# Split weights moved by 384 bytes, a seven-product scheme on two or four chunks by group, and plain products in the last two blocks

## The chip, the cores and the metric

The kernel runs on one core of a Trainium2 chip. The metric is the device time of one execution in microseconds (us). Before the change it is 1715.49 us, the median of three runs (1714.62 to 1716.32). The engines in this text are TensorE (PE; its weight loads, which overlap the matmuls, stand apart as PEld), VectorE (DVE), ScalarE (ACT), GpSimd (POOL) and SyncE (SP), which issues most DMAs. L132 is line 132 of the kernel before. On-chip memory (SBUF) has 128 partitions; an address is a byte offset within a partition. Matmuls accumulate in PSUM.

## The reference

One layer of a decoder for 256 tokens of width 2048 in float32: a combined projection, three token mixers (gated linear attention, stick-breaking attention, cross-attention into 256 memory tokens), a gated merge, an output projection, and a gated feed-forward block of width 5632.

```python
h = rmsnorm(x, attn_norm)
gq, gk, gv, gr, ga1, sq, sk, sv, mq, gates = split(h @ w_in)
y_gla = (rmsnorm(gla(gq, gk, gv, ga1)) * silu(gr)) @ w_br_gla
y_sb  = stick_breaking(rmsnorm(sq), rmsnorm(sk), sv) @ w_br_sb
y_mem = memory(rmsnorm(mq), rmsnorm(mem) @ w_mem_kv) @ w_br_mem
g = sigmoid(gates)                       # three gates of 2048 channels
x = x + (g0 * y_gla + g1 * y_sb + g2 * y_mem) @ w_o
gate, up = split(rmsnorm(x, ffn_norm) @ w_gate_up)
x = x + (silu(gate) * up) @ w_down
```

## The kernel before

**Tiling.** The 256 tokens are two tiles of 128 (t = 0, 1). A weight matrix is cut into blocks of 512 columns (NB) and chunks of 128 rows. One raw tile holds four chunks of one block (KG = 4), 1 MB, fetched by one DMA of SP.

**Split operands.** Every large product is done in a form of float32 with reduced precision (fp32r), three matmuls for one: a value is split into a high part and a low remainder, and high x high, high x low and low x high are added up in PSUM. The activations are split once (xTh and xTl, oh and ol, hh and hl, fh and fl). The weights are split as they arrive, two chunks (128 x 1024) at a time, a "half" of a raw tile: ACT casts raw to wh (L131), then DVE subtracts to get wl (L132). The split weights are the moving operand of a matmul (512 columns), the split activations the stationary one (128 columns).

**The rings.** Raw tiles and split tiles lie in rings at the upper end of SBUF: `widen("ring1", 3, 4)` opens three raw tiles and four pairs of wh and wl there, later calls add two raw tiles and two pairs. The rings lie below the top of SBUF one after the other, so that in the built program each raw, wh and wl begins at 480 modulo 512; the activations, their formed sums and the small tiles come from the lower end, and every stationary operand of a split matmul begins at 96 modulo 512. The first operand that a row names is the moving one, the second the stationary one.

**Two ways to multiply.** `gemm` does one block: for each half, two token tiles x two chunks x three matmuls (L196 to L198). `sgemm` does a pair of blocks. For the first eight chunks (two halves of SP = 4 chunks of the contraction) it treats tokens, contraction and columns as 2 x 2 blocks and forms the result from seven products in place of eight (Winograd's form of Strassen's scheme); the chunks behind the first eight go the plain way, in `rest`. The products are p1 to p3, q4 and p5 to p7. Four of them need sums of activations, made once for each stage by `make_forms` on DVE and ACT; three need sums of weights, which DVE makes in place in the raw tiles just ahead of the split (L246). `keep` copies a product out of PSUM on ACT, p7 and `result` combine the pieces on DVE (L294, L295, L297, L333). A group of a pair of blocks with 16 chunks has 84 matmuls of products and 96 of rest; one with 12 chunks has 84 and 48.

**The order.** The program is one stream. `seq` in `sgemm` lists products and rests; after each piece `step()` lets one item of a background list run, the transposes and splits of the next activations (`to_chunks`, transposes at L377) or the sums of `make_forms`. Each engine then works through its own instructions in order. The `late` variant of `seq` puts the products that need `forms` further back; it is used at a stage's first group.

**The stages**, in order: w_mem_kv; w_in (with w_ga at L700 to L702) and w_br_mem by `gemm`, with the attention in the background; then w_gate in pairs of blocks by `sgemm`, with w_br_sb and w_br_gla by `gemm`; w_o by `sgemm` (2 groups, 16 chunks); the feed-forward block in three parts of 4, 4 and 3 groups of w_gate_up (16 chunks each), each followed by 2 groups of w_down (16, 16 and 12 chunks). The first two parts add their w_down result to a tile in DRAM; the last one adds that tile, read back as x2s, and stores the output.

Of the kernel before, what the change touches and what calls it, by code (L numbers as in the profile page):

```python
# [9 lines left out]
F32 = mybir.dt.float32  # L10
# [64 lines left out]
def trunk(ctx: ExitStack, tc: tile.TileContext, a, out):  # L75
# [11 lines left out]
    def widen(name, raw, w):  # L87
# [2 lines left out]
        free_raw.extend([(pool, raw)] * raw)  # L90
        splits.extend([(pool, w)] * w)

    widen("ring1", 3, 4)
    small = ctx.enter_context(tc.tile_pool(name="small", bufs=2))
    main = ctx.enter_context(tc.tile_pool(name="main", bufs=1))
# [104 lines left out]
            k0 += n  # L200
        return o

    def sgemm(xs, forms, w, blks, row0=0, late=False, plus=None):

        nk = len(xs)
        o = {(t, j): acc() for t in range(2) for j in range(2)}
        x0, x1 = tmp(), tmp()
        c, q, loaded, begun = {}, {}, {}, set()

        def load(j, k):
            raw, done = loads()
            n = min(KG, nk - k)
            nc.sync.dma_start(raw[:, :n], w[blks[j], :, row0 + k : row0 + k + n])
            return raw, done

        def mm(dst, xp, wh, wl, last):

            xh, xl = xp
            pe.matmul(dst[:], xh, wh, start=id(dst) not in begun, stop=False, skip_group_check=True)  # L230
            begun.add(id(dst))
            pe.matmul(dst[:], xh, wl, start=False, stop=False, skip_group_check=True)  # L232
            pe.matmul(dst[:], xl, wh, start=False, stop=last, skip_group_check=True)  # L233

        def half(raw, g):
            wh, wl = (x[:].rearrange("p (k n) -> p k n", k=2) for x in parts())
            split(wh, wl, raw[:, g : g + 2])
            return wh, wl

        def prod(dst, left, b, last, *sums, gone=()):  # L240


            for g in (0, 2):
                for to, of in sums:
                    x, y = (q[i][0][:, g : g + 2] for i in (to, of))
                    dve.tensor_tensor(x, x, y, op=ALU.add)  # L246
                wh, wl = half(q[b][0], g)
                for i in range(2):
                    mm(dst, left[g + i], wh[:, i], wl[:, i], last and (g, i) == (2, 1))
                if g:  # L250
                    for i in gone:
                        q[i][1]()
                step()

        def single(h, t):
            return [[x[:, t * P : (t + 1) * P] for x in xs[h * SP + i]] for i in range(SP)]

        def formed(f):
            return [[x[:, f, i] for x in forms] for i in range(SP)]

        def keep(at):
            c[at] = piece()
            act.copy(c[at][:], x0[:])

        def p1():
            q[21] = load(0, SP)
            prod(x0, single(1, 0), 21, False)
            keep((0, 0))

        def p2(last):  # L270
            q[11] = load(0, 0)
            prod(o[0, 0], single(0, 0), 11, last)

        def p3(last):
            q[12] = load(1, 0)
            prod(o[0, 1], formed(0), 12, last)

        def q4(last):
            prod(o[1, 0], single(0, 1), 11, last, (11, 12), gone=(11, 12))

        def p5():
            q[22] = load(1, SP)
            prod(x1, formed(1), 21, True, (21, 22))

        def p6():

            prod(x0, formed(2), 12, False, (22, 12), (12, 21), gone=(21,))
            keep((0, 1))

        def p7():  # L290
            prod(x0, formed(3), 22, True, gone=(22,))
            keep((1, 0))
            c[1, 1] = piece()
            dve.tensor_tensor(c[1, 1][:], x1[:], c[1, 0][:], op=ALU.subtract)  # L294
            dve.tensor_tensor(c[0, 1][:], x1[:], c[0, 1][:], op=ALU.subtract)  # L295
            for at, p in (plus or {}).items():
                dve.tensor_tensor(c[at][:], c[at][:], p, op=ALU.add)  # L297

        def rest(j, k, last):

            if (j, k) not in loaded:
                raw, done = load(j, k)
                loaded.update({(j, k + g): (raw, g, done if g or k + 2 == nk else None) for g in (0, 2)})
            raw, g, done = loaded[j, k]
            wh, wl = half(raw, g)
            if done:
                done()
            for t in range(2):
                for i in range(2):
                    xp = [x[:, t * P : (t + 1) * P] for x in xs[k + i]]  # L310
                    mm(o[t, j], xp, wh[:, i], wl[:, i], (t, j) in last and i == 1)
            step()

        r0, r1 = ([(rest, j, k) for k in range(2 * SP, nk, 2)] for j in range(2))
        if late:
            seq = [(p1,), (p2,), *r0[:2], *r1[:2], (p5,), (p3,), *r0[2:3], (p6,), *r0[3:], (p7,), (q4,), *r1[2:]]
        else:
            seq = [x for n, p in enumerate((p1, p5, p3, p6)) for x in ((p,), *r0[n : n + 1])]
            seq += [(p2,), (p7,), *r1[:1], (q4,), *r1[1:]]
        into = {p2: [(0, 0)], p3: [(0, 1)], q4: [(1, 0)]}  # L320
        todo = [into.get(f[0], [(t, f[1]) for t in range(2)] if len(f) > 1 else []) for f in seq]
# [577 lines left out]
    for b, w_br in ((1, "w_br_sb"), (0, "w_br_gla")):  # L899
# [31 lines left out]
    for n0 in range(0, D, 2 * NB):  # L931
# [5 lines left out]
        for j, result in sgemm(ms, sm_, a["w_o"], (n0 // NB, n0 // NB + 1), late=n0 == 0, plus=plus):  # L937
# [26 lines left out]
    for part in (range(0, 4), range(4, 8), range(8, NF)):  # L964
        fs, tiles = [], []
        for i in part:
            for j, result in sgemm(hs, sf, a["w_gate_up"], (i, NF + i), late=i == 0):
                if j == 0:
                    g = [result(t) for t in range(2)]
                    for t in range(2):  # L970
# [13 lines left out]
        if final:  # L984

            x2s = [kit.tile([P, D], F32, tag=f"sf{x}", name="x2s", bufs=1) for x in "hl"]
            for t in range(2):
                nc.gpsimd.dma_start(x2s[t][:], x2d[:, t])
        for n0 in range(0, D, 2 * NB):
            plus = None  # L990
            if final:
                plus = {(t, j): x2s[t][:, n0 + j * NB : n0 + (j + 1) * NB] for t in range(2) for j in range(2)}
            blks = (n0 // NB, n0 // NB + 1)
            for j, result in sgemm(fs, sd, a["w_down"], blks, row0=4 * part[0], plus=plus):
                n = n0 + j * NB
                for t in range(2):
                    if not final:
                        nc.gpsimd.dma_start(x2d[:, t, n : n + NB], result(t), accum_op=ALU.add)
                        continue

                    width = NB // 2 if n + NB == D else NB
                    for c in range(0, NB, width):
                        v = result(t, cols=slice(c, c + width))
                        nc.sync.dma_start(out[t * P : (t + 1) * P, n + c : n + c + width], v)


# [45 lines left out]
```

## Time and profile before

| | |
|---|---|
| time, median of 3 runs | 1715.49 us |
| time of the profiled execution | 1714.35 us |
| its span, first to last instruction | 1712.6 us |
| mean granted TensorE clock | 0.994 |
| HBM read, written | 320.60 MB, 8.39 MB |

The profiled execution takes 1.75 us more than its span. Busy time says how long an engine had something in hand; matmuls are pipelined and overlap each other in the profile, so a PE that is busy for the whole of a stage can still differ in how far apart its matmuls start. In a group of instructions, "wl<-raw,wh 128x1024" names the tile written, the tiles read and partitions x elements; the number behind the bar is the sum of busy time, then the mean in ns of one, then the idle time of the engine ahead of them and who ended it.

### The profile page before, as it was taken

Reading aid. Unit: us, or ns where it says so; the run is one execution under the profiler, and the core shown is the slowest. Engines: PE = TensorE matmul, PEld = TensorE weight load, DVE = VectorE, ACT = ScalarE, POOL = GpSimd, SP = SyncE. Lnnn points to the kernel's source line nnn. Section 1 sums busy time; section 2 is a strip of 40 time slices with the busy share of each in tenths; the row PEclk is TensorE's granted clock in tenths of the full one; section 3 lists DMA queues with packets and bytes.
Section 4 is the critical chain, followed back from the end, with each engine's and each line's share of the span. In section 5 each row is a group of like instructions: output and inputs, shape, how many; then the busy total and the mean of one; then the engine's idle time right before and its main releaser. Section 6 shows DMA issues by size and latency. Waiting matters only on the chain.

```text
span 1712.6 us, 19224 instructions
## 1 busy us (share of the span) xinstructions
PE 1678.6 (98%) x7320; PEld 1344.5 (79%) x7320; DVE 1391.6 (81%) x1607; ACT 966.0 (56%) x1163; POOL 20.5 (1%) x32
## 2 busy tenths in 40 slices
PE   9999999999999999999999989999999999999997
PEld 6888888888777877888888767788888788888776
DVE  6756566664665578887999999999999999999998
ACT  7554444654643455655656656565566666566553
POOL 0000000000000000000000000000000000000000
PEclk9999999999999999999999999999999999999999
DMA  8765445445434557546546555465765455775363
GB/s 328 255 230 188 147 148 180 164 148 196 160 137 140 184 180 258 199 154 237 194 151 221 198 195 197 152 224 208 230 218 197 153 208 194 230 239 193 139 226 113
DMA packets 53756, 330.23 MB, mean 193 GB/s; under 512 B 5904, under 2 KB 10512, under 8 KB 15520
## 3 DMA queue, kind: packets, MB, share of 16 engines
q1 hardware_dynamic: 49968, 320.17, 53.0%
q0 software_dynamic: 3232, 8.39, 2.4%
q8 instruction: 57, 0.93, 0.2%
q10 hardware_dynamic: 464, 0.45, 0.1%
q14 instruction: 35, 0.29, 0.0%
HBM read 320.60 MB, written 8.39 MB: 192 GB/s over the span
## 4 chain that ended last, share of the span: by engine, by line
PE 86%; DVE 10%; ACT 2%; issue 1%; DMA 0%; SPq 0%; DVEq 0%; ACTq 0%
PE acc L196 12%; PE acc L197 12%; PE acc L198 12%; PE acc L232 11%; PE acc L230 11%; PE acc L233 11%; PE tmp L232 4%; PE tmp L233 4%; DVE wl L132 4%; PE tmp L230 4%; DVE raw L246 3%; ACT wh L131 1%; PE tmp L377 1%; DVE cv L343 1%; PE tmp L580 0%
## 5 line engine op out<-in xcount | busy, mean ns | idle before, releaser
L131 ACT CAST wh<-raw 128x1024 fp32r<-128x1024 f32 (+1 forms) x725 | 750.7, 1049 | 641.0 <-PE acc L198 294.4
L132 DVE TENSOR_TENSOR wl<-raw,wh 128x1024 fp32r<-128x1024 f32 (+1 forms) x725 | 866.5, 1218 | 238.6 <-ACT wh L131 236.2
L196 PE MATMUL acc<-wh,xTh 128*128 128x512 f32 x576 | 232.8, 404 | 0.0
L198 PE MATMUL acc<-wh,xTl 128*128 128x512 f32 x576 | 227.5, 395 | 0.0
L197 PE MATMUL acc<-wl,xTh 128*128 128x512 f32 x576 | 227.5, 395 | 0.0
L246 DVE TENSOR_TENSOR raw<-raw 128x1024 f32<-128x1024 f32 x184 | 219.7, 1218 | 1.0
L230 PE MATMUL acc<-wh,hh 128*128 128x512 f32 x440 | 174.6, 402 | 3.8 <-ACT wh L131 3.8
L232 PE MATMUL acc<-wl,hh 128*128 128x512 f32 x440 | 174.6, 397 | 0.8 <-DVE wl L132 0.7
L233 PE MATMUL acc<-wh,hl 128*128 128x512 f32 x440 | 174.1, 396 | 0.0
L196 PE MATMUL acc<-wh,oh 128*128 128x512 f32 x320 | 127.5, 400 | 1.9 <-ACT wh L131 1.1
L198 PEld LDWEIGHTS acc<-wh,xTl 128*128 128x128 f32 x576 | 108.4, 188 | 25.6 <-issue 0.3
L196 PEld LDWEIGHTS acc<-wh,xTh 128*128 128x128 f32 x576 | 108.6, 189 | 24.3 <-ACT wh L131 0.8
L197 PE MATMUL acc<-wl,oh 128*128 128x512 f32 x320 | 127.0, 397 | 0.5 <-DVE wl L132 0.5
L197 PEld LDWEIGHTS acc<-wl,xTh 128*128 128x128 f32 x576 | 108.6, 189 | 23.8 <-issue 0.7
L198 PE MATMUL acc<-wh,ol 128*128 128x512 f32 x320 | 127.2, 398 | 0.0
L230 PEld LDWEIGHTS acc<-wh,hh 128*128 128x128 f32 x440 | 83.2, 190 | 25.0 <-ACT wh L131 5.8
L232 PEld LDWEIGHTS acc<-wl,hh 128*128 128x128 f32 x440 | 83.3, 189 | 20.6 <-DVE wl L132 1.5
L233 PEld LDWEIGHTS acc<-wh,hl 128*128 128x128 f32 x440 | 83.1, 189 | 19.2
L232 PE MATMUL acc<-wl,fh 128*128 128x512 f32 x208 | 82.3, 397 | 2.3 <-DVE wl L132 2.3
L230 PE MATMUL acc<-wh,fh 128*128 128x512 f32 x208 | 81.8, 397 | 1.5 <-ACT wh L131 1.5
L233 PE MATMUL acc<-wh,fl 128*128 128x512 f32 x208 | 81.8, 395 | 0.0
L196 PEld LDWEIGHTS acc<-wh,oh 128*128 128x128 f32 x320 | 60.6, 190 | 18.4 <-ACT oh L134 1.7
(284 smaller groups left out, 2329.9 us busy)
## 6 DMA issues: line engine op xcount, KB each, us to landing
raw<-in_w_gate_up SPq DMA_DIRECT2D x88, 1024.0 KB, 5.0
raw<-in_w_in SPq DMA_DIRECT2D x72, 1024.0 KB, 4.9
raw<-in_w_down SPq DMA_DIRECT2D x44, 1024.0 KB, 4.9
raw<-in_w_gate SPq DMA_DIRECT2D x32, 1024.0 KB, 4.9
raw<-in_w_o SPq DMA_DIRECT2D x16, 1024.0 KB, 5.0
raw<-in_w_mem_kv SPq DMA_DIRECT2D x15, 1024.0 KB, 5.1
raw<-in_w_br_mem SPq DMA_DIRECT2D x8, 1024.0 KB, 5.1
raw<-in_w_br_sb SPq DMA_DIRECT2D x8, 1024.0 KB, 6.9
```

Of the source, the lines that this page charges most:

```text
L131: act.copy(hi, src)
L132: dve.tensor_tensor(lo, src, hi.bitcast(F32), op=ALU.subtract)
L196: pe.matmul(o[t][:], xh[:, s], wh[:, j], start=k == 0, stop=False)
L197: pe.matmul(o[t][:], xh[:, s], wl[:, j], start=False, stop=False)
L198: pe.matmul(o[t][:], xl[:, s], wh[:, j], start=False, stop=k == nk - 1)
L230: pe.matmul(dst[:], xh, wh, start=id(dst) not in begun, stop=False, skip_group_check=True)
L232: pe.matmul(dst[:], xh, wl, start=False, stop=False, skip_group_check=True)
L233: pe.matmul(dst[:], xl, wh, start=False, stop=last, skip_group_check=True)
L246: dve.tensor_tensor(x, x, y, op=ALU.add)
L343: dve.tensor_tensor(dst, a, b, op=op)
L377: pe.transpose(dst, src, ident)
```

## The change

There are three edits.

1. A tile of 96 float32 (384 bytes) that nothing reads or writes is placed at the upper end of SBUF ahead of the rings. All raw, wh and wl tiles move down by 384 bytes and begin at 96 modulo 512. Nothing else moves.
2. `sgemm` gets a number p, 4 or 2: how many of the four chunks of a half go through the seven products. With p = 2 the other two chunks of each of the four raw tiles go the plain way, by `rest`, right behind the product that fetched the tile (`fetch` notes them as loaded). p is 4 for w_gate, 2 for w_o, 2 for the even groups of w_gate_up and 4 for the odd ones, 2 for the first group of each w_down and 4 for the second.
3. In the last w_down, the second pair of blocks is done by `gemm`, one block after the other, and its sum with x2s is made in x2s itself.

```diff
+PAD = 96
...
+    pad = ctx.enter_context(tc.tile_pool(name="pad", bufs=1, side="right"))
+    pad.tile([P, PAD], F32, name="pad")
     widen("ring1", 3, 4)
...
-            for g in (0, 2):
+            for g in range(0, p, 2):
...
+        def fetch(i, j, k):
+            q[i] = load(j, k)
+            loaded.update({(j, k + g): (q[i][0], g, None) for g in range(p, SP, 2)})
...
+        w21, w22, w11, w12 = (
+            [(f,), *((rest, j, k + g) for g in range(p, SP, 2))]
+            for f, j, k in ((p1, 0, SP), (p5, 1, SP), (p2, 0, 0), (p3, 1, 0))
+        )
         if late:
-            seq = [(p1,), (p2,), *r0[:2], *r1[:2], (p5,), (p3,), *r0[2:3], (p6,), *r0[3:], (p7,), (q4,), *r1[2:]]
+            seq = [*w21, *w11, *r0[:2], *r1[:2], *w22, *w12, *r0[2:3], (p6,), *r0[3:], (p7,), (q4,), *r1[2:]]
...
-            for j, result in sgemm(hs, sf, a["w_gate_up"], (i, NF + i), late=i == 0):
+            for j, result in sgemm(hs, sf, a["w_gate_up"], (i, NF + i), 4 if i % 2 else 2, late=i == 0):
...
+            if final and n0 > 0:
+                for n in (n0, n0 + NB):
+                    o = gemm(fs, a["w_down"], n, row0=4 * part[0])
+
+                    def summed(t, cols):
+                        v = x2s[t][:, n + cols.start : n + cols.stop]
+                        dve.tensor_tensor(v, v, o[t][:, cols], op=ALU.add)
+                        return v
+
+
+                    stored(n, summed, NB // 2 if n + NB == D else NB)
+                continue
```

By count of the built programs, PE gets 78 matmuls more (6,732 of 512 columns with split weights become 6,810), DVE has 97 instructions less and ACT 42 casts less. The DMAs that bring weights stay as many.

On DVE, in the first group of the first part of w_gate_up, behind the last of its `forms`, there stood before (the raw<-raw rows are the in-place sums, the cv<-acc and cv<-tmp rows the combining of pieces):

```order
L132 TENSOR_TENSOR wl<-raw,wh 128x1024
L246 TENSOR_TENSOR raw<-raw 128x1024
L132 TENSOR_TENSOR wl<-raw,wh 128x1024 x4
L246 TENSOR_TENSOR raw<-raw 128x1024 x4
L132 TENSOR_TENSOR wl<-raw,wh 128x1024 x5
L246 TENSOR_TENSOR raw<-raw 128x1024 x2
L333 TENSOR_TENSOR cv<-acc,cv 128x512
L132 TENSOR_TENSOR wl<-raw,wh 128x1024 x2
L294 TENSOR_TENSOR cv<-tmp,cv 128x512
```

And now, from the last of the forms on (the lines are those of the changed kernel, where L137 is the split, L251 the sum, and L346, L303 and L304 the combining):

```order
L137 TENSOR_TENSOR sfl<-cv,sfh 128x512 x3
L137 TENSOR_TENSOR wl<-raw,wh 128x1024 x5
L251 TENSOR_TENSOR raw<-raw 128x1024 x3
L137 TENSOR_TENSOR wl<-raw,wh 128x1024 x6
L346 TENSOR_TENSOR cv<-acc,cv 128x512
L303 TENSOR_TENSOR cv<-tmp,cv 128x512
```

The run of four sums between two runs of splits has become one of three, and the single sum ahead of it is gone from this place.

On DVE at the end of the program, the second pair of blocks of the last w_down, before:

```order
L246 TENSOR_TENSOR raw<-raw 128x1024 x4
L132 TENSOR_TENSOR wl<-raw,wh 128x1024 x6
L297 TENSOR_TENSOR cv<-cv,x2s 128x512
L132 TENSOR_TENSOR wl<-raw,wh 128x1024
L246 TENSOR_TENSOR raw<-raw 128x1024
L294 TENSOR_TENSOR cv<-tmp,cv 128x512
L295 TENSOR_TENSOR cv<-tmp,cv 128x512
L297 TENSOR_TENSOR cv<-cv,x2s 128x512 x3
L132 TENSOR_TENSOR wl<-raw,wh 128x1024
L246 TENSOR_TENSOR raw<-raw 128x1024
L333 TENSOR_TENSOR cv<-acc,cv 128x512
L132 TENSOR_TENSOR wl<-raw,wh 128x1024 x2
```

And now (L1016 is the sum with x2s):

```order
L137 TENSOR_TENSOR wl<-raw,wh 128x1024 x7
L1016 TENSOR_TENSOR x2s<-x2s,acc 128x512 x2
L137 TENSOR_TENSOR wl<-raw,wh 128x1024
L1016 TENSOR_TENSOR x2s<-x2s,acc 128x256 x4
L1076 UNCONDITIONAL_BRANCH
```

The in-place sums and the combining of pieces have left this place; the splits stay, with one add for each half of a token tile behind them.

More of the change, by code (lines that the diff above doesn't have):

```diff
@@ L201, in gemm, with sgemm @@
         return o
-    def sgemm(xs, forms, w, blks, row0=0, late=False, plus=None):
+    def sgemm(xs, forms, w, blks, p, row0=0, late=False, plus=None):
         nk = len(xs)
@@ L248, in prod @@
                 for i in range(2):
-                    mm(dst, left[g + i], wh[:, i], wl[:, i], last and (g, i) == (2, 1))
-                if g:
+                    mm(dst, left[g + i], wh[:, i], wl[:, i], last and g + i == p - 1)
+                if g + 2 == p:
                     for i in gone:
@@ L263, in keep @@
             act.copy(c[at][:], x0[:])
+        def fetch(i, j, k):
+            q[i] = load(j, k)
+            loaded.update({(j, k + g): (q[i][0], g, None) for g in range(p, SP, 2)})
         def p1():
-            q[21] = load(0, SP)
+            fetch(21, 0, SP)
             prod(x0, single(1, 0), 21, False)
@@ L270, in p2 @@
         def p2(last):
-            q[11] = load(0, 0)
+            fetch(11, 0, 0)
             prod(o[0, 0], single(0, 0), 11, last)
         def p3(last):
-            q[12] = load(1, 0)
+            fetch(12, 1, 0)
             prod(o[0, 1], formed(0), 12, last)
@@ L281, in p5 @@
         def p5():
-            q[22] = load(1, SP)
+            fetch(22, 1, SP)
             prod(x1, formed(1), 21, True, (21, 22))
@@ L295, in p7 @@
             dve.tensor_tensor(c[0, 1][:], x1[:], c[0, 1][:], op=ALU.subtract)
-            for at, p in (plus or {}).items():
-                dve.tensor_tensor(c[at][:], c[at][:], p, op=ALU.add)
+            for at, more in (plus or {}).items():
+                dve.tensor_tensor(c[at][:], c[at][:], more, op=ALU.add)
         def rest(j, k, last):
@@ L314, in sgemm @@
         r0, r1 = ([(rest, j, k) for k in range(2 * SP, nk, 2)] for j in range(2))
+        w21, w22, w11, w12 = (
+            [(f,), *((rest, j, k + g) for g in range(p, SP, 2))]
+            for f, j, k in ((p1, 0, SP), (p5, 1, SP), (p2, 0, 0), (p3, 1, 0))
+        )
         if late:
-            seq = [(p1,), (p2,), *r0[:2], *r1[:2], (p5,), (p3,), *r0[2:3], (p6,), *r0[3:], (p7,), (q4,), *r1[2:]]
+            seq = [*w21, *w11, *r0[:2], *r1[:2], *w22, *w12, *r0[2:3], (p6,), *r0[3:], (p7,), (q4,), *r1[2:]]
         else:
-            seq = [x for n, p in enumerate((p1, p5, p3, p6)) for x in ((p,), *r0[n : n + 1])]
-            seq += [(p2,), (p7,), *r1[:1], (q4,), *r1[1:]]
+            seq = [*w21, *r0[:1], *w22, *r0[1:2], *w12, *r0[2:3], (p6,), *r0[3:], *w11, (p7,), *r1[:1], (q4,), *r1[1:]]
         into = {p2: [(0, 0)], p3: [(0, 1)], q4: [(1, 0)]}
@@ L905, in trunk @@
             k = (b * D + n0) // NB
-            for _, result in sgemm(xs, sx, a["w_gate"], (k, k + 1), late=b == 1 and n0 == 0):
+            for _, result in sgemm(xs, sx, a["w_gate"], (k, k + 1), 4, late=b == 1 and n0 == 0):
                 gs.append([result(t) for t in range(2)])
@@ L936, in trunk @@
         plus = {(t, j): xr[j][:, t] for t in range(2) for j in range(2)}
-        for j, result in sgemm(ms, sm_, a["w_o"], (n0 // NB, n0 // NB + 1), late=n0 == 0, plus=plus):
+        for j, result in sgemm(ms, sm_, a["w_o"], (n0 // NB, n0 // NB + 1), 2, late=n0 == 0, plus=plus):
             if x2 is None:
@@ L988, in trunk, with stored @@
                 nc.gpsimd.dma_start(x2s[t][:], x2d[:, t])
-        for n0 in range(0, D, 2 * NB):
+        def stored(n, result, width=NB):
+            for t in range(2):
+                for c in range(0, NB, width):
+                    v = result(t, slice(c, c + width))
+                    nc.sync.dma_start(out[t * P : (t + 1) * P, n + c : n + c + width], v)
+        for n0 in range(0, D, 2 * NB):
+            if final and n0 > 0:
[7 more added lines that the diff above has]
+                continue
             plus = None
@@ L993, in trunk @@
             blks = (n0 // NB, n0 // NB + 1)
-            for j, result in sgemm(fs, sd, a["w_down"], blks, row0=4 * part[0], plus=plus):
+            for j, result in sgemm(fs, sd, a["w_down"], blks, 4 if n0 else 2, row0=4 * part[0], plus=plus):
                 n = n0 + j * NB
+                if final:
+                    stored(n, lambda t, cols: result(t, cols=cols))
+                    continue
                 for t in range(2):
[L997 to L1004, printed above, removed]
+                    nc.gpsimd.dma_start(x2d[:, t, n : n + NB], result(t), accum_op=ALU.add)
 def kernel(**inputs):
```

## The prediction

> **What bounds the kernel now.** The first view is the page: busy shares, and the chain of work that ended last.
>
> ```profile
> span 1712.6 us, 19224 instructions
> PE 1678.6 (98%) x7320; PEld 1344.5 (79%) x7320; DVE 1391.6 (81%) x1607; ACT 966.0 (56%) x1163; POOL 20.5 (1%) x32
> PE 86%; DVE 10%; ACT 2%; issue 1%; DMA 0%; SPq 0%; DVEq 0%; ACTq 0%
> ```
>
> TensorE (PE) is on the chain for 86%, VectorE (DVE) for 10%, DMA for nothing. Where the 10% lie is told by busy time in the stages that the change edits: w_o, then three parts of gate_up, the first two each followed by w_down, and the last w_down.
>
> ```profile
> core 0: us, PE busy (x) PEld busy (x) DVE busy (x) ACT busy (x) POOL busy (x), PEclk, DMA share, GB/s
> 882.90:973.10 90.20, 88.76 (x401) 71.47 (x400) 86.23 (x94) 57.69 (x76) 3.40 (x6) 1.00 0.61 216
> 973.10:1161.60 188.50, 178.58 (x756) 141.00 (x755) 181.26 (x208) 112.92 (x135) 1.08 (x2) 0.97 0.51 181
> 1161.60:1246.10 84.50, 84.50 (x369) 68.58 (x368) 80.46 (x78) 49.77 (x52) 5.31 (x7) 1.00 0.68 218
> 1246.10:1421.50 175.40, 172.23 (x745) 138.81 (x744) 167.29 (x168) 107.42 (x118) 1.53 (x2) 0.99 0.56 195
> 1421.50:1506.10 84.60, 84.60 (x370) 68.62 (x369) 80.01 (x77) 49.89 (x52) 5.33 (x7) 1.00 0.68 218
> 1506.10:1638.60 132.50, 129.44 (x557) 103.90 (x556) 126.06 (x128) 80.90 (x89) 2.61 (x4) 0.99 0.60 210
> 1638.60:1712.60 74.00, 64.53 (x273) 49.81 (x271) 67.61 (x73) 35.43 (x39) 0.00 (x0) 1.00 0.40 130
> ```
>
> The two middle w_down stages have PE busy throughout: 360 matmuls of 512 columns and 8 transposes in 84.5 us. Elsewhere PE is idle at times, with DVE at 96% (181.26 of 188.50). Busy time understates the loss, so each stage is priced from the distance between matmul starts.
>
> ```profile
> 559.72 0.39 PE L197 MATMUL acc<-wl,xTh 128*128 128x512 f32 x1
> ...
> 560.18 0.40 PE L196 MATMUL acc<-wh,xTh 128*128 128x512 f32 x1
> 560.42 0.40 PE L197 MATMUL acc<-wl,xTh 128*128 128x512 f32 x1
> ...
> 562.98 0.39 PE L196 MATMUL acc<-wh,xTh 128*128 128x512 f32 x1
> ```
>
> ```profile
> 252.99 0.60 PE L377 MATMUL tmp<-cst,sq 128*128 128x128 f32 x4
> 253.35 0.48 PE L196 MATMUL acc<-wh,xTh 128*128 128x512 f32 x1
> ```
>
> The first and the last row of the first piece are 14 intervals apart: 3.26/14 = 0.2329 us a matmul. Four transposes take 0.36 us, 0.09 each. The w_down stage confirms it: (84.5 - 8 x 0.09)/360 = **0.2327 us**. With the matmuls of the code (180 a group of 16 chunks, 132 of 12), the time beyond unbroken matmuls is: w_o 90.2 - 360 x 0.2327 - 40 x 0.09 = 2.8; first gate_up 188.5 - 167.5 - 32 x 0.09 = 18.1; second 175.4 - 167.5 - 2.2 = 5.7; third 132.5 - 125.7 - 1.4 = 5.4; last w_down 74.0 - 61.4 - 0.7 = 11.9. Of the last, 4.8 us is the tail behind the final matmul, started at 1707.60: sums, stores and landing.
>
> ```profile
> 1707.60 0.40 PE L233 MATMUL acc<-wh,fl 128*128 128x512 f32 x1
> ```
>
> That leaves 7.1, and 39.1 us in the five stages. Its cause stands in the waits of PE in the first gate_up, and in the order of time at 1350:
>
> ```profile
> PE tmp L230 <- ACT wh L131: 4.4, 5, 2.1
> PE acc L230 <- ACT wh L131: 3.1, 3, 1.6
> PE tmp L232 <- DVE wl L132: 1.6, 2, 1.1
> PE acc L232 <- DVE wl L132: 0.7, 1, 0.7
> ```
>
> ```profile
> 1349.76 1.21 DVE L246 TENSOR_TENSOR raw<-raw 128x1024 f32<-128x1024 f32 x1
> ...
> 1350.79 4.84 ACT L131 CAST wh<-raw 128x1024 fp32r<-128x1024 f32 x5 [1.20 <-PE tmp L233]
> ...
> 1352.84 0.49 PE L230 MATMUL tmp<-wh,sfh 128*128 128x512 f32 x1 [2.13 <-ACT wh L131]
> ```
>
> PE waits for split weights; ScalarE (ACT), named there, had itself waited, and DVE comes from an in-place sum. DVE is the late one. The granted clock of the first gate_up is 0.97; what the clock loses behind the waits is in its 18.1 and goes with them.
>
> **The sums that go.**
>
> ```profile
> L132 DVE TENSOR_TENSOR wl<-raw,wh 128x1024 fp32r<-128x1024 f32 (+1 forms) x725 | 866.5, 1218 | 238.6 <-ACT wh L131 236.2
> L246 DVE TENSOR_TENSOR raw<-raw 128x1024 f32<-128x1024 f32 x184 | 219.7, 1218 | 1.0
> L297 DVE TENSOR_TENSOR cv<-cv,x2s 128x512 f32<-128x512 f32 x8 | 5.1, 682 | 0.0
> ```
>
> With p = 2, a group's in-place sums fall from 8 to 4 and its split halves by 3 (seven products on two chunks become four plain ones): 7 x 1.218 = 8.5 us of DVE less, 3 casts of ACT less, 6 matmuls more (+1.4 us of PE). That holds for 2 groups of w_o, 6 of gate_up, 3 of w_down. The two ordinary last blocks lose 8 sums, 6 split halves and 6 combining adds: 14 x 1.218 + 6 x 0.682 = 21.1 us of DVE, for 12 matmuls (+2.8). PE gets 78 matmuls, 78 x 0.2327 = **+18.1 us**, all on the path: nothing covers them. DMA traffic is the same: a half's raw tile is still one load; it is held until the product that last reads it, as before.
>
> What comes back of the 39.1 us? In the first gate_up DVE falls to 181.26 - 17.1 = 164.2, against 167.5 + 2.9 + 2.8 = 173.2 of PE: 95%, the share at which the middle w_down stage loses nothing (80.46 of 84.5). But this stage begins behind w_o, with late transposes and forms, and its second and fourth group keep eight sums. The bounds are 0 and all 18.1; I leave 5. Second: 150.2 against 172.5; third: 109.0 against 129.9; both 87% or less, so I leave 1 of 5.7 and 1 of 5.4. The last stage: 67.6 - 8.5 - 21.1 = 38 against 66, so 0.5 of 7.1 remains; the tail of sums and stores stays. w_o: 69 against 90; 1 of 2.8. The two middle w_down stages had nothing to give back and pay 1.4 each. ACT has slack everywhere (112.92 of 188.50). In sum 18.1 + 8.5 - 39.1 = **-12.5 us** (first gate_up -10.3, last w_down -2.4, second -1.9, third -1.6, w_o +1.0, the middle w_down +2.8). If nothing stays lost, -21; if half of it does, -1.4. What is late next is PE itself.
>
> **The padding.** It moves raw, wh and wl by 384 bytes. In the built program's addresses the moving operand (wh, wl) stands at 480 modulo 512 and every stationary operand at 96; now both at 96. No split matmul of before has this relation, so its price is bounded by rows with others. The w_ga matmuls have the roles turned: stationary at 480, moving at 96, 256 columns.
>
> ```profile
> 404.81 0.28 PE L700 MATMUL tmp<-xTh,wh 128*128 128x256 f32 x1
> ...
> 408.96 0.28 PE L702 MATMUL tmp<-xTh,wl 128*128 128x256 f32 x1
> ```
>
> ```profile
> L233 PEld LDWEIGHTS acc<-wh,fl x208: 187/188/192, 1165.2 to 1707.4; 128*128 128x128 f32 x104
> ```
>
> ```profile
> L580 PEld LDWEIGHTS tmp<-mkT,mv_mqT x32: 187/190/192, 174.6 to 208.6; 128*128 128x128 f32 x32
> L580 PE MATMUL tmp<-mkT,mv_mqT x32: 377/379/381, 174.8 to 208.9; 128*128 128x256 f32 x32
> ```
>
> ```profile
> 174.84 1.89 PE L580 MATMUL tmp<-mkT,mv_mqT 128*128 128x256 f32 x8
> ```
>
> Of w_ga, 35 intervals take 4.15 us: 0.1186 for 256 columns, 0.463 ns a column against 0.2327/512 = 0.455. Two unlike placements, 2% apart, and part of that is what each matmul costs whatever its width. The third kind, plain float32 with both operands at 96, takes (1.89 - 0.38)/7 = 0.216 us a record; its 256 columns go through in more than one pass, so this is an end of the range and not a like case. Nearest is w_ga, so I take **0** for the padding, with 0.216 as the lower end; the upper, 0.24, is the longest step between matmuls in the piece at 560 us (560.18 to 560.42).
>
> [...]
>
> **The rivals.**
> - *The padding shortens each matmul a little.* 2 to 6 ns on 6,810 matmuls is 14 to 41 us: 1661 to 1688. For it: a column costs 0.455 ns where the float32 record shows that PE can go on every 0.216 us. Against: 480 and 96 swapped changes nothing of that size.
> - *It takes the whole excess away*: 0.2327 - 0.216 = 0.0167 x 6,810 = 114 us, down to 1588. DVE would follow: its total is 1391.6 - 115 = 1277. [...]
> - *The padding costs: slower than before.* [...] At 0.24 us that is 6,810 x 0.0073 = 50 us, 1752; half of it 1727. It outweighs the relief from 12.5/6,810 = 1.8 ns a matmul on. Against it: with both operands at 96, the weight load of L580 takes 190 ns (the middle of its three figures), and that of a split matmul with 480 against 96 takes 188.
> - *The relief doesn't arrive.* The waits stay because the sums still come in clumps (three in a row in the first group, the order shows); half of them kept gives 1713, all of them 1732.
>
> **How the numbers follow.** The profiled execution took 1714.35 us, 1.1 below the median of the three runs. From it: 1714.35 - 12.5 = **1702 us**, own range 1693 to 1713. Chances: this 0.47; a little shorter matmul 0.22; the whole excess or most of it 0.13; the padding costs 0.10; relief missing 0.08. The range 1645 to 1719 leaves out most of the third, and the upper part of the last two, about 0.2. Faster or slower means by more than 0.2% (3.4 us), about what a measurement of this kernel can tell from no change. Faster: 0.47 + 0.22 + 0.13 = 0.82. Slower: 0.08 of the padding's 0.10 and 0.03 of the missing relief: 0.11. Within: what is left of these two, 0.07.
>
> **What would show it.** Starts of 512-column matmuls 0.233 us apart at 560 us, where no other part of the change acts: the padding does nothing; anything but that decides between the rivals. The first gate_up near 178 us with DVE at 164, PE's waits there under 3 us; the middle w_down at 85.9; the last stage near 71.6. If the starts are unchanged and the first gate_up still takes 188 us, the step on DVE relief is wrong.

## The result, and the profile after

| | before | after |
|---|---|---|
| time, median of 4 runs each | 1715.12 us | 1662.85 us (1660.39 to 1663.44) |
| ratio, 95% interval | | 0.9692 (0.9675 to 0.9708) |
| time of the profiled execution | 1714.35 us | 1660.39 us |
| its span | 1712.6 us | 1658.6 us |
| mean granted TensorE clock | 0.994 | 1.000 |

The change takes 52.3 us off the median, 54.0 off the profiled execution; the forecast was 12.5. The page of the profile after, with its busy shares and the chain by engine:

```profile
span 1658.6 us, 19253 instructions
PE 1647.8 (99%) x7398; PEld 1352.2 (82%) x7398; DVE 1287.8 (78%) x1510; ACT 927.6 (56%) x1121; POOL 20.6 (1%) x32
PE 94%; DVE 4%; DMA 1%; ACT 1%; issue 0%; ACTq 0%; DVEq 0%
```

There are 78 matmuls more, and yet PE is busy 30.8 us less. DVE's part of the chain has gone from 10% to 4%. The starts of matmuls at 559 us, in order of time, where the padding alone acts:

```profile
559.29 0.39 PE L201 MATMUL acc<-wh,xTh 128*128 128x512 f32 x1
...
562.46 0.39 PE L203 MATMUL acc<-wh,ol 128*128 128x512 f32 x1
```

From the first row to the last are 14 intervals: 3.17/14 = 0.2264 us, against 0.2329 before. Next, busy time by stage, in the stages of the prediction (w_o, gate_up, w_down, gate_up, w_down, gate_up, last w_down; the columns are those of the prediction's table):

```profile
865.50:954.40 88.90, 88.90 (x412) 73.60 (x411) 71.11 (x79) 51.48 (x69) 3.40 (x6) 1.00 0.63 219
954.40:1125.10 170.70, 170.54 (x767) 140.24 (x766) 166.94 (x196) 107.51 (x129) 1.08 (x2) 1.00 0.54 200
1125.10:1209.00 83.90, 83.90 (x375) 69.47 (x374) 72.05 (x70) 47.08 (x49) 5.16 (x6) 1.00 0.68 219
1209.00:1377.90 168.90, 168.90 (x758) 139.80 (x758) 152.37 (x155) 101.49 (x112) 1.73 (x2) 1.00 0.58 203
1377.90:1461.80 83.90, 83.90 (x376) 69.45 (x375) 72.37 (x71) 47.09 (x49) 5.14 (x6) 1.00 0.69 219
1461.80:1588.80 127.00, 127.00 (x569) 105.16 (x568) 112.05 (x115) 75.19 (x83) 2.86 (x4) 1.00 0.61 220
1588.80:1658.60 69.80, 65.32 (x291) 53.52 (x290) 40.71 (x46) 25.40 (x27) 0.00 (x0) 1.00 0.38 136
```

PE is now without a gap in w_o, both middle w_down and two parts of gate_up, and the clock is whole. Worked out as in the prediction, the mean step of a w_down is (83.9 - 8 x 0.09)/366 = **0.2273 us** (before 0.2327). The first gate_up keeps one wait of PE, of 0.2 us in all:

```profile
PE tmp L390 <- DVE cv L988: 0.2, 1, 0.2
```

So two things happened: 6,810 matmuls became shorter by 0.2327 - 0.2273 = 5.4 ns, 36.8 us together, and the waits for split weights went from these stages. The experiments take these apart.

### The profile page after: what moved, and what is told of

Same layout as the page of the kernel before. It is cut to its first block, busy times and chain, and to the rows that moved or that the text cites. A ratio compares the mean times of both kernels' runs of the same rounds, so it can differ in the third digit from the quotient of the medians.

```text
span 1658.6 us, 19253 instructions
## 1 busy us (share of the span) xinstructions
PE 1647.8 (99%) x7398; PEld 1352.2 (82%) x7398; DVE 1287.8 (78%) x1510; ACT 927.6 (56%) x1121; POOL 20.6 (1%) x32
## 4 chain that ended last, share of the span: by engine, by line
PE 94%; DVE 4%; DMA 1%; ACT 1%; issue 0%; ACTq 0%; DVEq 0%
PE acc L238 13%; PE acc L237 13%; PE acc L235 13%; PE acc L201 13%; PE acc L203 13%; PE acc L202 13%; PE tmp L237 3%; PE tmp L238 3%; PE tmp L235 3%; DVE wl L137 2%; PE tmp L390 2%; DVE raw L251 1%; DVE cv L356 1%; DMA raw<-in_w_gate_up 0%; ACT wh L136 0%; PE tmp L621 0%
## 5 line engine op out<-in xcount | busy, mean ns | idle before, releaser
L136 ACT CAST wh<-raw 128x1024 fp32r<-128x1024 f32 (+1 forms) x686 | 714.9, 1051 | 637.5 <-PE acc L203 284.5
L137 DVE TENSOR_TENSOR wl<-raw,wh 128x1024 fp32r<-128x1024 f32 (+1 forms) x686 | 824.6, 1219 | 283.6 <-ACT wh L136 278.2
L201 PE MATMUL acc<-wh,xTh 128*128 128x512 f32 x576 | 230.3, 400 | 0.0
L235 PE MATMUL acc<-wh,hh 128*128 128x512 f32 x512 | 200.0, 391 | 0.0
L238 PE MATMUL acc<-wh,hl 128*128 128x512 f32 x512 | 199.5, 390 | 0.0
L237 PE MATMUL acc<-wl,hh 128*128 128x512 f32 x512 | 199.4, 389 | 0.0
L251 DVE TENSOR_TENSOR raw<-raw 128x1024 f32<-128x1024 f32 x132 | 159.9, 1219 | 5.0 <-DMA raw<-in_w_gate_up 3.1
L237 PEld LDWEIGHTS acc<-wl,hh 128*128 128x128 f32 x512 | 96.2, 188 | 20.1 <-DVE wl L137 0.3
L238 PEld LDWEIGHTS acc<-wh,hl 128*128 128x128 f32 x512 | 96.1, 188 | 20.0
L235 PEld LDWEIGHTS acc<-wh,hh 128*128 128x128 f32 x512 | 96.2, 188 | 19.6
L235 PE MATMUL acc<-wh,fh 128*128 128x512 f32 x220 | 85.9, 391 | 0.1
L201 PEld LDWEIGHTS acc<-wh,oh 128*128 128x128 f32 x320 | 60.6, 189 | 15.5 <-ACT oh L139 1.7
```

The source lines that it names most:

```text
L136: act.copy(hi, src)
L137: dve.tensor_tensor(lo, src, hi.bitcast(F32), op=ALU.subtract)
L201: pe.matmul(o[t][:], xh[:, s], wh[:, j], start=k == 0, stop=False)
```

## The experiments

All times below are medians beside runs of the kernel before on the same chip (1716.2 to 1716.5 us); three kernels of the program were timed once, which is said there. "Distance" is the start of the moving operand less that of the stationary one. Stage times are those of the profiled execution.

### Each part alone

The question is how much of the 52 us belongs to the padding and how much to the relief of DVE. First the kernel before with the pad alone:

```diff
+    pad = ctx.enter_context(tc.tile_pool(name="pad", bufs=1, side="right"))
+    pad.tile([P, 96], F32, name="pad")
     widen("ring1", 3, 4)
```

> The kernel before with the padding alone: raw, wh and wl at 96 modulo 512, products as before. Theory A (place): the step between 512-column matmuls falls from 0.2325 to 0.2267 us as in the changed kernel, because moving and stationary operand begin at the same place. The first 883 us hold about 3,400 such matmuls, so some 19 us come from there; in the feed-forward block DVE is at 96 to 100% already, so little is added: 1690 us, between 1680 and 1697. Theory B (the step follows from fewer sums, splits and waits, not from the place): the step stays 0.2325 and the time 1715, within 3 us.

Measured: 1685.42 us (1682.96 to 1687.73), ratio 0.9813 (0.9797 to 0.9829). Busy time of w_o, the first gate_up and the first w_down, and PE's waits in that gate_up:

```profile
870.00:959.00 89.00, 87.25 (x401) 71.23 (x400) 86.13 (x94) 57.61 (x76) 3.39 (x6) 1.00 0.61 219
959.00:1143.90 184.90, 174.61 (x755) 140.43 (x754) 180.80 (x208) 113.17 (x135) 1.08 (x2) 0.97 0.52 185
1143.90:1226.50 82.60, 82.60 (x369) 68.38 (x369) 80.01 (x78) 49.75 (x52) 5.13 (x6) 1.00 0.68 223
```

```profile
PE tmp L232 <- ACT wh L133: 4.4, 4, 2.2
PE acc L232 <- ACT wh L133: 3.2, 2, 1.6
PE tmp L234 <- DVE wl L134: 1.7, 2, 1.0
PE acc L234 <- DVE wl L134: 0.9, 2, 0.6
```

The w_down stage, in which PE never waits, has gone from 84.5 to 82.6 us: (82.6 - 0.72)/360 = 0.2274 us a matmul, the step of after. The first gate_up got 3.6 us shorter, about its 720 x 5.3 ns = 3.8, and its waits are those of before: the padding does nothing for them.

Then the change without the pad:

```diff
-    pad = ctx.enter_context(tc.tile_pool(name="pad", bufs=1, side="right"))
-    pad.tile([P, PAD], F32, name="pad")
```

> The changed kernel without the padding: wh and wl at 480 again, the products on 2 or 4 chunks and the ordinary last blocks kept. Theory A: the step is 0.2325 again, 6,810 x 0.0058 = 39 us more than the changed kernel's 1662.9: 1702, between 1697 and 1706; this is also what the prediction gave for the change without any effect of the padding. Theory B: the step is 0.2267 and the time stays at 1663, within 3 us.

Measured: 1697.58 us (1695.55 to 1698.13), ratio 0.9887 (0.9872 to 0.9901); the profiled execution took 1697.52. This is the kernel that the prediction worked out, since it priced the padding at nothing. The first gate_up, the first w_down and the last w_down:

```profile
974.80:1148.50 173.70, 173.70 (x767) 141.19 (x765) 165.47 (x193) 107.19 (x128) 0.99 (x2) 1.00 0.54 197
1148.50:1234.70 86.20, 86.20 (x375) 69.51 (x374) 72.21 (x70) 47.00 (x49) 5.16 (x6) 1.00 0.67 214
1624.40:1695.70 71.30, 66.89 (x291) 53.72 (x289) 40.65 (x46) 25.36 (x27) 0.00 (x0) 1.00 0.38 133
```

PE is busy for all of the 173.70 us: not one wait is left there. Without the pad the step is that of before (its 512-column matmuls start 232.6 ns apart in the mean). So the padding sets the step and the other two edits remove the waits; alone they bring 30.8 and 18.6 us, together 52.3, some 3 more than their sum. With the other edits in place the pad brings 1697.58 - 1662.85 = 34.7 us.

### What it is about the place

The change speaks of the same place modulo 512 bytes. If that is the condition, a pad of 128 bytes (weights at 352, activations at 96, distance 256) must lose the gain.

```diff
-PAD = 96
+PAD = 32
```

> The changed kernel with a padding of 128 bytes in place of 384: wh and wl at 352 modulo 512 against 96. Theory A in its strict form (only the same place is fast): a step of 0.2325 and 1702 us. Theory A in a loose form (only 480 against 96 is slow, or the step varies with the distance): a step between 0.2267 and 0.2325 or beyond, 1663 to 1702. Theory B: 0.2267 and 1663.

Measured, one run: 1663.59 us, with a mean step of 227.2 ns. The same place modulo 512 isn't needed; half of that already does it.

To see the whole pattern, a kernel of matmuls alone: rows of 48 matmuls in fp32r, back to back, both operands in place beforehand. The stationary one begins at 96 modulo 512 and the moving one is put 32 bytes further from row to row.

```diff
+    def run(o, s, m, n, count=48):
+        return [(o[:, :n], S[:, s + 128 * (i % 4) : s + 128 * (i % 4) + 128], M[:, m + 512 * (i % 2) : m + 512 * (i % 2) + n], i == 0, i == count - 1) for i in range(count)]
...
+    qaa = run(warm, 120, 120, 512)
+    [pe.matmul(o, s, m, start=b, stop=e) for o, s, m, b, e in qaa]
+    qba = run(warm, 120, 0, 512)
```

> The kernel does nothing of the reference: it loads x, rounds parts of it, and runs rows of 48 matmuls with the moving operand at a given place modulo 512 and the stationary one at another, nothing else going on. First the stationary at 96 and the moving at 96, 128, 160 and so on up to 64 (16 rows of 512 columns), then both at one place elsewhere, other pairs, fewer columns, and the two pairs of the kernels again. Theory A: steps of 0.2267 at the same place and 0.2325 at 480 against 96, with the curve between them showing which distances are slow. Theory B: all rows of 512 columns have the same step, within 1 ns.

Five of its rows in order of time; a row is 48 matmuls, and its first column is its start. The moving operand of L51 begins at 320, that of L53 at 352, of L55 at 384, of L61 at 480, of L63 at 0:

```profile
101.70 11.35 PE L51 MATMUL warm<-M,S 128*128 128x512 f32 x48
112.89 11.05 PE L53 MATMUL warm<-M,S 128*128 128x512 f32 x48
123.78 11.37 PE L55 MATMUL warm<-M,S 128*128 128x512 f32 x48
...
157.19 11.36 PE L61 MATMUL warm<-M,S 128*128 128x512 f32 x48
168.39 11.40 PE L63 MATMUL warm<-M,S 128*128 128x512 f32 x48
```

From start to start, L53 at 352 takes 10.89 us, 226.9 ns a matmul; L51 at 320 takes 11.19, 233.1 ns; L61, the relation of the kernel before (480 against 96), takes 11.20, 233.3 ns. All places, by the distance (mean between starts within each row, ns):

| distance, bytes | 0 | 32 | 64 | 96 | 128 | 160 | 192 | 224 |
|---|---|---|---|---|---|---|---|---|
| moving at 96 to 320 | 227.2 | 233.4 | 229.1 | 233.6 | 233.4 | 234.1 | 233.2 | 233.2 |
| 256 further on | 226.8 | 233.4 | 229.1 | 233.6 | 233.4 | 234.1 | 233.2 | 233.2 |

The two lines are alike: the pattern repeats every **256 bytes**. Further rows had both operands at 0, 256, 352 or 480: 226.7 to 227.2. With fewer columns (distance 0, 128, 256):

| columns | 0 | 128 | 256 |
|---|---|---|---|
| 128 | 110.5 | 111.6 | 111.6 |
| 256 | 121.0 | 118.7 | 119.9 |
| 384 | 173.5 | 176.1 | 173.4 |
| 512 | 227.2 | 233.4 | 226.8 |

At 256 columns a distance of 128 costs nothing; at 384 it costs 2.6 ns and at 512 some 6.

Two more kernels test the pattern in the whole program. A pad of 64 bytes gives distance 320, which is 64 modulo 256, the middle value of the table:

```diff
-PAD = 96
+PAD = 16
```

> The changed kernel with a padding of 64 bytes: wh and wl at 416 modulo 512, 320 behind the stationary operand at 96, 64 modulo 256. Theory A (the distance modulo 256 sets the step, as the rows of bare matmuls say: 229.1 ns at 64): 6,810 x 2.4 ns = 16 us above the changed kernel, 1679, between 1675 and 1683. Theory B (only the two kernels' places or the bare matmuls have this): 1663 or 1698.

Measured, one run: 1674.55 us, mean step 229.04 ns; the bare rows have 229.1. From the step of after, 227.2, it is (229.04 - 227.2) x 6,810 = 12.5 us, and 1662.85 + 12.5 = 1675.4. The range expected, 1675 to 1683, went by 2.4 ns a matmul and was a little high. And the same distance made at the other end: the weights stay at 480, the activations move up by 128 bytes to 224.

```diff
+    pad = ctx.enter_context(tc.tile_pool(name="pad", bufs=1))
+    pad.tile([P, 32], F32, name="pad")
...
-    pad = ctx.enter_context(tc.tile_pool(name="pad", bufs=1, side="right"))
-    pad.tile([P, PAD], F32, name="pad")
```

> The changed kernel with no padding at the upper end and 128 bytes at the lower end instead: raw, wh and wl stay at 480 as in the kernel before, the activations and all other tiles move to 224, 256 bytes away. Theory A (the distance between the two operands of a matmul counts, not the place of either, nor the place at which DVE and ACT work): a step of 0.2267 and 1663, within 3 us. Theory B (480 as such is a bad place for the split weights): 0.2325 and 1698.

Measured, one run: 1661.43 us, step 227.19 ns. It is the distance that counts, not where the weights lie.

What of the matmul is it? The author's guess, ahead of these rows: the load of the next stationary operand hinders the moving stream. Then fewer stationary columns must take away a part of the penalty at a bad distance, and a part of the step at a good one. A second kernel of bare rows has that, places that alternate from matmul to matmul, odd distances, and other types:

```diff
+    qba = run(warm, 120, 120, 512, 96, 0, 0, S, M)
...
+    qha = run(warm, 0, 0, 512, 128, 32, 0, S, M)
...
+    qra = run(warm, 0, 0, 512, 128, 0, 0, S2, M2)
```

> Nothing of the reference again: rows of 48 matmuls of 512 columns. First fewer stationary columns (128, 96, 64, 32) at the same place and at 128 bytes apart; then rows in which only the stationary, only the moving, or both change by 128 bytes from matmul to matmul; small distances (4, 8, 16, 64, 192, 240, 252 bytes); bfloat16 at distances of 0, 64, 128, 192 bytes; plain float32 at 0 and 128. [...] Theory M (the moving operand's own place counts, or the stream is slow by itself): the same step at every number of stationary columns. [...]

| rows of 512 columns | ns a matmul |
|---|---|
| 128, 96, 64, 32 stationary columns, distance 0 | 227.2, 230.0, 229.9, 231.7 |
| 96, 64, 32 stationary columns, distance 128 | 231.7, 229.4, 230.8 |
| distance 4, 8, 16, 240, 252 | 236.6, 231.5, 231.7, 236.6, 230.2 |
| stationary, moving, both alternate by 128 | 232.2, 230.1, 228.3 |
| bfloat16, distance 0, 64, 128, 192 | 216.1, 215.8, 215.8, 215.8 |
| plain float32, distance 0, 128, for each record | 429.2, 429.2 |

One half of that guess falls and the other holds. At distance 0 fewer stationary columns don't shrink the step, they lengthen it, from 227.2 to 229.9 to 231.7 ns. But the penalty of distance 128 does shrink: it is 233.4 - 227.2 = 6.2 ns with 128 columns, 1.7 with 96, and with 64 and 32 the row at distance 128 is even 0.4 and 0.9 shorter than that at distance 0. The alternating rows leave it open too. Where only one operand alternates, every other matmul has its own operands 128 bytes apart, and the mean of 227.2 and 233.4 is 230.3; the rows have 232.2 and 230.1. Where both alternate, each matmul has its own operands at distance 0, and the stationary operand of the next one is 128 away: 228.3, nearer to 227.2 than to 233.4. So the place of the next stationary operand can't be the whole cause.

The distance matters in neither of the other types at the distances run: bfloat16 has 215.8 to 216.1 ns, plain float32 429.2 a record at both, in two records a matmul (96 for the 48 of a row). The bfloat16 rows, at distances 0, 64, 128 and 192; the first three take 10.37, 10.36 and 10.36 us from start to start:

```profile
212.29 10.53 PE L77 MATMUL warm<-Mb,Sb 128*128 128x512 bf16 x48
222.66 10.52 PE L79 MATMUL warm<-Mb,Sb 128*128 128x512 bf16 x48
233.02 10.52 PE L81 MATMUL warm<-Mb,Sb 128*128 128x512 bf16 x48
243.38 10.52 PE L83 MATMUL warm<-Mb,Sb 128*128 128x512 bf16 x48
```

### What the relief rests on

The change with p = 4 everywhere keeps the pad and the plain last blocks. If p = 2 is what removes the waits, they come back; if the last blocks or the pad did it, they don't.

```diff
-        for j, result in sgemm(ms, sm_, a["w_o"], (n0 // NB, n0 // NB + 1), 2, late=n0 == 0, plus=plus):
+        for j, result in sgemm(ms, sm_, a["w_o"], (n0 // NB, n0 // NB + 1), 4, late=n0 == 0, plus=plus):
...
-            for j, result in sgemm(hs, sf, a["w_gate_up"], (i, NF + i), 4 if i % 2 else 2, late=i == 0):
+            for j, result in sgemm(hs, sf, a["w_gate_up"], (i, NF + i), 4, late=i == 0):
...
-            for j, result in sgemm(fs, sd, a["w_down"], blks, 4 if n0 else 2, row0=4 * part[0], plus=plus):
+            for j, result in sgemm(fs, sd, a["w_down"], blks, 4, row0=4 * part[0], plus=plus):
```

> The changed kernel with p = 4 in all groups, padding and ordinary last blocks kept. Theory A (the relief of DVE by p = 2 counts for the three gate_up stages, as in the prediction's step on DVE): those stages and the w_down between them go back to the durations of the padding alone (89.0, 184.9, 82.6, 172.4, 82.6, 131.2 us) and the last stage stays near 69: about 1681, between 1677 and 1685. Theory B (most of the relief is from the ordinary last blocks and the new order): within 5 us of the changed kernel's 1663.

Measured: 1682.0 us (1676.69 to 1684.42), ratio 0.9794 (0.9775 to 0.9813), 19.2 us above the change. The first gate_up of it, and PE's waits there:

```profile
956.90:1143.10 186.20, 175.15 (x755) 140.56 (x754) 181.01 (x208) 113.09 (x135) 1.08 (x2) 0.97 0.51 184
```

```profile
PE tmp L235 <- ACT wh L136: 4.9, 5, 2.2
PE acc L235 <- ACT wh L136: 3.3, 3, 1.6
PE tmp L237 <- DVE wl L137: 2.0, 2, 1.3
PE acc L237 <- DVE wl L137: 0.9, 2, 0.6
```

DVE is back at 181.01 us, the waits at 11.1 us, the clock at 0.97, and the stage takes 15.5 us more than in after, with fewer matmuls. So p = 2 carries the relief. Edit 3 by itself, the change with its last pair of blocks back on `sgemm`:

```diff
-            if final and n0 > 0:
+            if False:
```

> The changed kernel with the last pair of blocks done by the seven products on four chunks, as before; padding and p kept. 12 matmuls less, 12 x 0.2267 = 2.7 us, and 21 us of DVE more in a stage of 69.8 us in which DVE has 43 now. Theory A: DVE at 64 of 67 us, waits of 2 to 6 us come back at the end: 1662 to 1667, no more than 4 us from the changed kernel. Theory B (the ordinary blocks were worth the whole 7.1 us of waits that the prediction counted): 1667 to 1670.

Measured: 1664.26 us (1662.69 to 1665.23), ratio 0.9692 (0.9676 to 0.9708). The stage:

```profile
1592.20:1663.50 71.30, 63.68 (x279) 51.00 (x277) 59.73 (x64) 32.27 (x36) 0.00 (x0) 0.99 0.38 133
```

It is 71.3 us against 69.8: the plain last blocks bring 1.5 us in their stage, which the medians can't tell from nothing.

Are all the groups with p = 2 needed, now that the waits are gone? Each one costs 6 matmuls, 1.4 us. This kernel takes it from the second group of w_o, from two of the six of gate_up (groups 6 and 10, the second with p = 2 in the second part and in the third), and from w_down. Its pad is 128 bytes, which leaves the step as it is.

```diff
-PAD = 96
+PAD = 32
...
-        for j, result in sgemm(ms, sm_, a["w_o"], (n0 // NB, n0 // NB + 1), 2, late=n0 == 0, plus=plus):
+        for j, result in sgemm(ms, sm_, a["w_o"], (n0 // NB, n0 // NB + 1), 4 if n0 else 2, late=n0 == 0, plus=plus):
...
-            for j, result in sgemm(hs, sf, a["w_gate_up"], (i, NF + i), 4 if i % 2 else 2, late=i == 0):
+            for j, result in sgemm(hs, sf, a["w_gate_up"], (i, NF + i), 2 if i in (0, 2, 4, 8) else 4, late=i == 0):
...
-            for j, result in sgemm(fs, sd, a["w_down"], blks, 4 if n0 else 2, row0=4 * part[0], plus=plus):
+            for j, result in sgemm(fs, sd, a["w_down"], blks, 4, row0=4 * part[0], plus=plus):
```

> The changed kernel with a padding of 128 bytes and p = 2 in fewer groups: the first of w_o, groups 0, 2, 4 and 8 of gate_up, none of w_down. 36 matmuls less, 36 x 0.2267 = 8.2 us, and 51 us of DVE more, spread over stages in which DVE has 8 to 17 us to spare each. Theory A (PE is the bound in those stages and DVE may rise to 97%): 1655, between 1653 and 1659. Theory B (waits come back as soon as DVE passes some 95%): 1660 to 1670.

Measured: 1671.84 us (1671.0 to 1673.9), ratio 0.9741 (0.9726 to 0.9755), slower than the change by 9.0 us and above both of the ranges expected. The first w_down, the second gate_up and the last w_down, and PE's longest waits in the gate_up:

```profile
1131.90:1214.40 82.50, 82.50 (x369) 68.28 (x368) 78.85 (x76) 50.06 (x52) 5.13 (x6) 1.00 0.69 223
1214.40:1388.00 173.60, 170.00 (x752) 139.54 (x751) 160.24 (x162) 104.24 (x115) 1.73 (x2) 0.99 0.56 197
1598.80:1672.10 73.30, 66.78 (x285) 53.28 (x283) 50.64 (x55) 28.48 (x32) 0.00 (x0) 0.96 0.43 144
```

```profile
PE tmp L235 <- ACT wh L136: 2.1, 1, 2.1
PE tmp L237 <- DVE wl L137: 1.0, 1, 1.0
```

The middle w_down is cheaper by 1.4 us, as hoped: it had nothing to be relieved of. But the second gate_up, with one group of p = 2 in place of two, takes 173.6 against 168.9, although DVE has work for only 92% of it. A stage can wait for DVE with its mean well below full. The last w_down, whose first group lost p = 2 too, takes 73.3 against 69.8, with DVE at 69%. The other three stages, w_o and the first and third gate_up, take 1.2 to 1.7 us more each.

That points to the places where p = 2 is wasted (the middle w_down) and where it is needed. In after, PE's waits for split weights between 500 us and w_o all lie in the first group of w_gate, which has p = 4; the profile of after, for that group:

```profile
605.50:654.10 48.60, 44.91 (x197) 34.98 (x196) 48.44 (x57) 32.34 (x41) 0.00 (x0) 1.00 0.59 213
```

```profile
PE tmp L237 <- DVE wl L137: 1.5, 2, 0.9
PE tmp L235 <- ACT wh L136: 0.8, 1, 0.8
PE acc L235 <- ACT wh L136: 0.7, 2, 0.5
PE acc L237 <- DVE wl L137: 0.6, 2, 0.5
```

```diff
-            for _, result in sgemm(xs, sx, a["w_gate"], (k, k + 1), 4, late=b == 1 and n0 == 0):
+            for _, result in sgemm(xs, sx, a["w_gate"], (k, k + 1), 2 if b == 1 and n0 == 0 else 4, late=b == 1 and n0 == 0):
...
-            for j, result in sgemm(fs, sd, a["w_down"], blks, 4 if n0 else 2, row0=4 * part[0], plus=plus):
+            for j, result in sgemm(fs, sd, a["w_down"], blks, 2 if final and n0 == 0 else 4, row0=4 * part[0], plus=plus):
```

> The changed kernel with p = 2 also in the very first group of w_gate, whose 5.7 us beyond unbroken matmuls were left alone by the change, and p = 4 in the first group of w_down in parts one and two, which lose nothing. Theory A (waits behind DVE in a stage's first group go with p = 2; w_down takes DVE at 98% without a loss, as in the padding alone): some 4 us back in w_gate for 1.4 of matmuls, 2 x 1.4 us of matmuls saved: 1658, between 1655 and 1660. Theory B (the DVE work added in w_down comes back as waits in the gate_up behind it, as with fewer groups on p = 2): 1661 to 1667.

Measured: **1658.11 us** (1655.95 to 1658.51), ratio 0.9659 (0.9643 to 0.9676), 4.7 us below the change and the fastest of all; each of its four runs is below each of the change's. The same group of w_gate, the first w_down and the second gate_up:

```profile
606.90:651.10 44.20, 44.20 (x203) 36.32 (x203) 41.12 (x51) 29.56 (x39) 0.00 (x0) 1.00 0.62 230
1123.40:1206.00 82.60, 82.60 (x370) 68.35 (x369) 78.96 (x76) 50.05 (x52) 5.13 (x6) 1.00 0.69 223
1206.00:1374.80 168.80, 168.80 (x758) 139.75 (x757) 153.16 (x156) 101.52 (x112) 1.73 (x2) 1.00 0.58 203
```

The w_gate group gets 4.4 us shorter with six matmuls more, and each middle w_down 1.3. The second gate_up, behind a w_down with p = 4 as in the kernel just above, is back at 168.8: what lengthened it there was its own group 6 and not the work of DVE in the w_down before it.

## Why the prediction was wrong in size

**The step that failed** is the price of the padding: "Nearest is w_ga, so I take **0** for the padding". Worked out from the step it is 36.8 us; measured, it is 34.7 with the other edits in place and 30.8 without them. The forecast of -12.5, these -36.8 and the 4.5 that the first gate_up gave beyond the forecast come to -53.8, and the profiled execution lost 54.0. Two things went wrong in that one reading. The w_ga rows were taken as an unlike placement because stationary and moving are swapped; the runs show that the distance modulo 256 sets the step, to about 1 ns (226.7 to 227.5 at 0, 228.8 to 229.1 at 64, 232.7 to 233.4 at 128), and 96 - 480 and 480 - 96 are both 128 modulo 256. By that they were the same slow kind. And w_ga has 256 columns, where the bare rows show no penalty at any of three distances (w_ga takes 118.6 ns, the bare row at distance 128 takes 118.7); the division by columns (0.463 against 0.455 ns) hid that, since a matmul's time isn't in proportion to its columns: from 256 to 384 to 512 columns at distance 256 (119.9, 173.4, 226.8) it grows by 53.4 to 53.5 ns, 0.417 a column, and 226.8 - 512 x 0.417 leaves 13.3 that don't grow, an estimate from these three rows alone (the row of 128 columns, at 111.6, lies above their line). The right reading of the before trace was that no row of it could price the padding.

**The rivals.** What came is the first one in kind: 2 to 6 ns shorter, with 5.4 measured, 1661 to 1688; the prediction gave it 0.22. The range of 1645 to 1719 holds the result because of this rival; the sum's own range, 1693 to 1713, doesn't. The whole excess didn't go: the lower end of 0.216 is what bfloat16 reaches (215.8 to 216.1 ns), and no fp32r row here is below 226.7. That the padding costs fell, and with it the sign: the same place is the fast one (226.7 to 227.2 ns in the bare rows). The price of 0.24 does nearly exist at other distances (236.6 ns at 4 bytes). That the place is worth nothing, as the prediction took it, agrees with the bfloat16 and plain float32 rows (215.8 to 216.1 ns, 429.2 a record) and is contradicted for fp32r, where the rows lie up to 10 ns apart (226.7 to 236.6). "The relief doesn't arrive" fell too: without the pad there are no waits left in the first gate_up.

**The relief of DVE** was right in mechanism and too small. Without the pad it was forecast at -12.5, and measured at -16.8 in the profiled execution (1714.35 to 1697.52) and -18.6 in the medians. By stage, in us:

| | before | forecast | e2, no pad | after |
|---|---|---|---|---|
| w_o | 90.2 | 91.2 | 90.8 | 88.9 |
| first gate_up | 188.5 | 178.2 | 173.7 | 170.7 |
| first w_down | 84.5 | 85.9 | 86.2 | 83.9 |
| second gate_up | 175.4 | 173.5 | 173.1 | 168.9 |
| second w_down | 84.6 | 86.0 | 86.3 | 83.9 |
| third gate_up | 132.5 | 130.9 | 130.3 | 127.0 |
| last w_down | 74.0 | 71.6 | 71.3 | 69.8 |

Six of the seven are within 0.6 us. The mis-sized term is "The bounds are 0 and all 18.1; I leave 5" of the first gate_up: nothing was left, though DVE's 165.47 us there are 1.3 above the forecast 164.2. The cost of the 78 matmuls and the gain in the last stage were right; of the latter, 1.5 us is all that edit 3 can be seen to bring in the final kernel.

**Why together more than the sum.** Perhaps the padding brings less where DVE is late. From the seven stages of the table it takes 18.6 us when the relief is there (e2 to after: 1.9, 3.0, 2.3, 4.2, 2.4, 3.3 and 1.5), and 13.7 when it isn't (before to the pad alone); the third gate_up, for one, fell by 3.3 us in the first case and by 1.3 in the second. The 4.9 us between them is more than the 2.9 by which the medians exceed the sum; runs of one kernel differ by that much (1682.96 to 1687.73 with the pad alone). And ahead of w_o, where the two kernels with the pad are the same program, one profiled execution came to w_o at 870.0 us and the other at 865.5. So neither the surplus nor its cause is shown.

**Open**: why 256 bytes, and where the 13.3 ns estimated at the best place come from. Fewer stationary columns took the penalty of distance 128 away, but lengthened the step at the best place, and no other cause was tried.

## What to carry to other kernels

Where a trace holds one placement only, no row of it prices another: measure it with bare rows of the same type and width, which cost one short run here and would have turned the forecast. For fp32r matmuls of 512 columns, begin the moving and the stationary operand a multiple of 256 bytes apart: that gave 226.7 to 227.5 ns a matmul here, the other distances run 228.8 to 236.6. Relieve an engine in the groups in which PE is seen to wait for it, not where its mean share is high: the middle w_down lost nothing at 95% of DVE, while the second gate_up lost 4.7 us at 92% and the last w_down 3.5 us at 69%.

## What the runs showed of the hardware

- An fp32r matmul of 512 columns with a stationary operand of 128 starts 226.7 to 227.5 ns after the last one where its operands begin a multiple of 256 bytes apart, 228.8 to 229.1 at 64 bytes off and 230.2 to 236.6 at the other distances run; at 256 columns no such penalty was seen (121.0, 118.7 and 119.9 at distances 0, 128 and 256). With 64 or 32 stationary columns, distances 0 and 128 lie within 1 ns of each other (229.4 to 231.7). Bfloat16 (215.8 to 216.1 at distances 0 to 192) and plain float32 (429.2 a record at 0 and 128) show no difference at 512.
- With the pad alone, the longest single wait of PE in the first gate_up is 2.2 us, and yet the granted clock falls to 0.50 there twice, for 3.4 and 6.7 us, once behind a run of shorter waits and once behind that longest one (the two rows below, the clock being the number behind POOL's). The trace before has the same in its first gate_up: 0.50 for 3.4 us from 1005.4 us on, behind idle times of PE of 0.91 and 1.59 us, and for some 6.7 us from 1090.8 us on, behind 2.13 and 1.09 us. With the waits gone it is 1.00 in the whole stage (after, and the change without the pad). In the trace before, at a clock of 0.50, six matmuls start 2.13/5 = 0.426 us apart (1006.21 to 1008.34 us), against 0.2327 at 1.00. At such a step these 10 us do some 5 us of work, an estimate from the two rows and these starts: part of what the waits cost is the slow clock behind them.

```profile
991.40:994.80 3.40, 3.40 (x10) 2.66 (x9) 3.40 (x4) 0.00 (x0) 0.00 (x0) 0.50 0.63 195
1073.40:1080.10 6.70, 5.55 (x11) 3.46 (x12) 6.70 (x7) 3.89 (x4) 0.00 (x0) 0.50 0.44 143
```
